# Reading the moving columns of all long matmuls as two alternating halves

## The chip, the core and the metric

The kernel runs on one core of one Trainium2 chip. TensorE multiplies, VectorE and ScalarE do elementwise work, GpSimd does a little of it and issues some transfers, SyncE issues most transfers, and 16 DMA engines move the data. The metric is the device time of one execution in microseconds (us). Before the change it is 2804.27 us, the median of three runs (2803.52 to 2804.97).

A TensorE product has two operands. The stationary one, 128 by 128 here and called the weights of the array, is loaded first; the moving one is streamed through column by column, and each of its columns gives one column of output in PSUM. The profile has a row for each of the two steps: LDWEIGHTS on "PEld", MATMUL on "PE".

## What is computed

One layer of a hybrid encoder trunk on 256 prompt tokens and 8 x 16 sample tokens, 384 in all, with a model width of 2048. In short:

```python
proj = rmsnorm(x) @ w_in                    # pool | z | xBC | dt | gates
a_pool = windowed means of pool - pool, mapped by pool_w, scaled by pool_scale
xbc = silu(causal_conv(xbc)); dt = softplus(dt_raw + dt_bias)
y, h = ssd_scan(xh, dt, A, Bm, Cm, h0)      # 64 heads, 8 groups
a_ssd = gated_rmsnorm(y + d_skip * xh, z)
merged = sigmoid(g_A) * (a_pool @ w_pool_proj) + sigmoid(g_B) * (a_ssd @ w_ssd_proj)
x = x + rmsnorm(merged @ w_out)
x = x + rmsnorm(square(relu(rmsnorm(x) @ w_up)) @ w_down)
```

All inputs and outputs are float32. The outputs are the new tokens and the new pool, convolution and SSD states of both groups.

## The kernel before

**Three matmuls for each product.** Each float32 operand is split into a rounded high part `h` (ScalarE, type fp32r) and the remainder `l` (VectorE, fp32r). A product is h·h + h·l + l·h, three matmuls that add up in the same PSUM columns. Each weight unit is a 128 x 1024 tile: SyncE fetches it (`wfetch`, L61), ScalarE and VectorE split it (`wsplit`, L70 and L71), and three such tiles are in flight.

**Two kinds of long product.** In the first, the tokens move: the output is a tile of 128 channels by 384 tokens, the stationary operand is a 128 x 128 block of weights, and the moving one is a tile of 128 input channels by 384 tokens. `mm3` (L82 to L85) issues the three matmuls, `half` (L91) runs eight such triples on one weight unit, `proj` (L111) runs two units into one PSUM tile. The columns of `w_in` for pool, z and xBC, the maps `pool_w`, the few columns for dt, and `w_up` go this way; `eprod` (L278) does the first four pool tiles while the inputs arrive, and `prod` and `prod_back` (L1128, L1146) the first `w_up` tiles, of which the first two are partly taken in pieces of 256 and 128 tokens.

In the second, the weights move: the output is 128 tokens by 512 channels, the stationary operand is a 128 x 128 block of tokens, and the moving one is 512 columns of a weight unit. `moving` (L117) runs these: in a unit there are two blocks of 128 rows, three token blocks and three matmuls, 18 in all (L125 to L127). The two gate parts of `w_in`, `w_pool_proj`, `w_ssd_proj`, `w_out` and `w_down` go this way. `_moving` (L1328) lays these weights out on the host.

**Stages.** Pool tiles and dt come first, then gate A and the pool output, then the SSD stage. That stage has eight groups of ten `proj` products (six for xBC, four for z), and between them come short SSD products in plain fp32 and fp32r (`t_trx`, `t_cb`, `t_Y`, `t_yi`, `t_pp`, `t_su`) which `lump` puts at set places in TensorE's order. Then follow gate B, the SSD output with the merging (`merge`, transposes at L916), `w_out`, and the MLP: in each of eight rounds eight `w_up` tiles and then four `w_down` blocks.

**Order.** Every engine runs its instructions in the order in which the program has them. `behind` ties an instruction behind another, `later` puts it behind the latest weight split, and `chain` ties consecutive products together. The program's tiles set the waits.

**Who reads the PSUM tiles of the first kind.** `pool_tile` multiplies by the token scale `rstd` into a window buffer (L355 for the 256 prompt tokens, L356 for the samples, each behind its 15 kept rows). `conv_in` writes into a buffer of 24 segments of 16 tokens, each behind 3 kept columns (L550). `zproj` multiplies by `rstd` (L881). `pool_map` scales and splits (L406, L407). The dt product is taken out at L448 and L450, and the `w_up` tiles at L1252. `proj` alternates two PSUM banks; the other products take turns in six.

Of the kernel before, what the change touches and what calls it, by code (L numbers as in the profile page):

```python
# [14 lines left out]
P = 128  # L15
T = 384
TP = 256
NB = 8
# [15 lines left out]
def build(ctx, tc, io):  # L34
# [44 lines left out]
    def wload(src, name):  # L79
        return wsplit(wfetch(src, name))  # L80

    def mm3(out, wh, wl, xh, xl, first, last, **how):  # L82
        te.matmul(out, wh, xh, start=first, stop=False, **how)  # L83
        te.matmul(out, wh, xl, start=False, stop=False, **how)  # L84
        return te.matmul(out, wl, xh, start=False, stop=last, **how)  # L85
# [31 lines left out]
    def moving(o, units, lhs, tail, done, pool=None, own=0, hook=None, mid=None):  # L117
        nk = 2 * len(units)
        n = len(units)

        def mm(b, wh, wl, k, k2):
            t = slice(b * P, b * P + P)
            c = slice(k2 * 512, k2 * 512 + 512)
            mh, ml = lhs[k][0][:, t], lhs[k][1][:, t]
            te.matmul(o[b], mh, wh[:, c], start=k == 0, stop=False)  # L125
            te.matmul(o[b], mh, wl[:, c], start=False, stop=False)  # L126
            last[0] = te.matmul(o[b], ml, wh[:, c], start=False, stop=k == nk - 1)  # L127

        for kp in range(n - tail):
            wh, wl = take(*units[kp])  # L130
            with behind(last[0] if chain[0] else None):
                for k2 in range(2):
                    for b in range(3):
                        mm(b, wh, wl, kp * 2 + k2, k2)
            if hook and kp in hook:
                hook[kp]()
        w = [wload(*units[kp]) for kp in range(n - tail, n - own)]
        for kp in range(n - own, n):
            f, name = wfetch(*units[kp])
            h = pool.tile([P, 1024], F32R, name=f"eh_{name}")  # L140
            l = pool.tile([P, 1024], F32R, name=f"el_{name}")
            s.activation(h, f, AF.Copy)
            v.tensor_tensor(l, f, h.bitcast(F32), ALU.subtract)
            w.append((h, l))
        for b in range(3):
            for i, (wh, wl) in enumerate(w):
                if mid and (b, i) in mid:
                    mid[b, i]()
                with behind(last[0] if mid else None):
                    for k2 in range(2):  # L150
                        mm(b, wh, wl, (n - tail + i) * 2 + k2, k2)
            done(b)
# [125 lines left out]
    def eprod(k, j, hl):  # L278
        h, l = hl
        col = lambda n: slice(j * 512 + n * P, j * 512 + n * P + P)  # L280
        xh, xl = xg[k]
        if k < 2:
            seq = [(0, h, xh), (0, h, xl)] if k == 0 else [(0, h, xh)]
            seq += [(n, h, xh) for n in range(1, 4)]
            seq += [(n, h, xl) for n in range(1 - k, 4)]
            seq += [(n, l, xh) for n in range(4)]
            for n, a, b in seq:
                with behind(last[0]):
                    last[0] = te.matmul(early[n], a[:, col(n)], b, start=k == 0 and a is h and b is xh, stop=False)
# [45 lines left out]
    with tc.tile_pool(name="phc", bufs=1, reuse_waits="tile") as pc, tc.tile_pool(name="phc2", bufs=2, reuse_waits="tile") as pc2:  # L335
# [12 lines left out]
        def pool_tile(gi, k4):  # L348
            w = WINDOWS[gi]
            k = gi * 4 + k4  # L350
            ps = early[k] if k < 5 else proj(in_units(1 + k), xg, f"p{k}")
            bf = bufs[k % 2]
            pv = bf[:, 15:271]
            sv = bf[:, 271:].rearrange("p (b t) -> p b t", b=NB)
            v.tensor_tensor(pv, ps[:, :TP], rstd[:, :TP], ALU.mult)  # L355
            v.tensor_tensor(  # L356
                sv[:, :, 15:],
                ps[:, TP:].rearrange("p (b t) -> p b t", b=NB),
                rstd[:, TP:].rearrange("p (b t) -> p b t", b=NB),
                ALU.mult,  # L360
            )
# [24 lines left out]
            v.tensor_tensor(d[:, :16], cur[:, 15:31], rc, ALU.mult)  # L386
            v.tensor_tensor(d[:, :16], d[:, :16], pv[:, :16], ALU.subtract)
            h = pc.tile([P, T], F32R, tag=f"dh{k4}", name=f"dh{k}", bufs=1)
            l = pc.tile([P, T], F32R, tag=f"dl{k4}", name=f"dl{k}", bufs=1)
            s.activation(h, d, AF.Copy)  # L390
            v.tensor_tensor(l, d, h.bitcast(F32), ALU.subtract)
            dd[gi][k4] = (h, l)

        def pool_map(gi, after=None):
            for hf in range(2):
                h, l = wload(io["pool_w"][gi, hf], f"pw{gi}_{hf}")
                for n2 in range(2):
                    n = gi * 4 + hf * 2 + n2
                    o = sstile(f"pw{n}")[:, :T]
                    with behind(after):  # L400
                        for k in range(4):
                            c = slice((n2 * 4 + k) * P, (n2 * 4 + k + 1) * P)
                            mm3(o, h[:, c], l[:, c], dd[gi][k][0], dd[gi][k][1], k == 0, k == 3)
                    ah, al = A[n]
                    sc = vec[:, V_PSC + n : V_PSC + n + 1]
                    s.activation(ah, o, AF.Copy, scale=sc)  # L406
                    v.scalar_tensor_tensor(  # L407
                        out=al, in0=o, scalar=sc, in1=ah.bitcast(F32), op0=ALU.mult, op1=ALU.subtract
                    )

        def gate_a(nb):
# [18 lines left out]
        def dt_phase(pb):  # L430
            ps = mmtile("pj_dt")[:, :T]
            for q in range(2):
# [5 lines left out]
                v.tensor_tensor(hl[:, :, 1], wv, hl[:, :, 0].bitcast(F32), ALU.subtract)  # L438
                for k in range(8):
                    c = hl[:, k].rearrange("p a n -> p (a n)")  # L440
                    te.matmul(ps, c, xg[q * 8 + k][0], start=q + k == 0, stop=False)
                    te.matmul(ps, c, xg[q * 8 + k][1], start=False, stop=q * 8 + k == KD - 1)
# [5 lines left out]
            with behind(s.copy(raw, ps[NH:])):  # L448
                s.activation(nA, alog, AF.Exp)
            v.tensor_tensor(raw, ps[:NH], raw, ALU.add)  # L450
# [78 lines left out]
    with tc.tile_pool(name="phd", bufs=2, reuse_waits="tile") as pd, tc.tile_pool(  # L529
# [15 lines left out]
        def conv_in(ui, c):  # L545
# [1 line left out]
            b = cbuf[ncv[0] % 3]  # L547
            ncv[0] += 1
            with later():
                v.tensor_tensor(b[:, :, 3:], seg(ps), seg(rstd), ALU.mult)  # L550
# [271 lines left out]
        for g in range(G + 1):  # L822
# [54 lines left out]
            def zproj(j):  # L877
                ps = proj(in_units(u0 + 6 + j), xg, f"z{g}_{j}")
                z = pd.tile([P, T], F32, tag="zs", name=f"zs{g}_{j}", bufs=7)
                with later():  # L880
                    v.tensor_tensor(z, ps, rstd, ALU.mult)  # L881
                    s.activation(z, z, AF.Silu)
                D.zs.append(z)

# [113 lines left out]
    with tc.tile_pool(name="phf", bufs=1, side="right", reuse_waits="tile") as pf, tc.tile_pool(  # L998
# [237 lines left out]
    with tc.tile_pool(name="phg", bufs=1, reuse_waits="tile") as pg, tc.tile_pool(  # L1236
# [9 lines left out]
        for c8 in range(NC):  # L1246
            hh = []
            for f8 in range(8):
                f = c8 * 8 + f8
                ps = ups[f] if f < 3 else proj([io["w_up"][f, 0], io["w_up"][f, 1]], xs2, f"up{f}")  # L1250
                t = pg2.tile([P, T], F32, tag="t", name=f"ht{f}")
                v.scalar_tensor_tensor(out=t, in0=ps, scalar=0.0, in1=r2, op0=ALU.max, op1=ALU.mult)  # L1252
# [163 lines left out]
```

## Time and profile before

| what | value |
|---|---|
| median of three runs | 2804.27 us |
| span of the profiled execution, first to last instruction | 2801.6 us |
| TensorE clock granted, mean | 0.999 |
| busy: TensorE matmul / weight load | 2791.7 / 2543.0 us |
| busy: VectorE / ScalarE / GpSimd | 1505.4 / 1171.9 / 135.1 us |
| matmuls | 15,269 |
| DMA traffic | 451.35 MB |

The device time of the profiled execution itself is not given apart from its span; the three timed runs have a median 2.7 us above that span. Rows of matmuls overlap, because one begins to stream while the one before still drains, and their ends are modelled; the distance between two starts is what a matmul costs in a full stream. The chain of waits is read in order of time, each piece with its start, its length and the number of instructions merged in it.

### The profile page before, as it was taken

What the parts mean: (1) busy time and instruction counts of PE and PEld (TensorE: products, weight loads), DVE (VectorE), ACT (ScalarE), POOL (GpSimd) and SP (SyncE); (2) the same over time, 40 slices, a digit from 0 to 9 for tenths busy, and PEclk for the clock granted to TensorE, in tenths of its full rate; (3) what the DMA queues carried; (4) which work ended last, traced back from release to release, by engine and by line L of the source; (5) the groups of instructions that cost most, each with busy time, mean ns of one, the idle gap of its engine ahead of it and who ended that gap; (6) DMA issues with size and microseconds to landing.
All of it is one profiled execution on the core that took longest, in us unless ns stands there. A gap on an engine that the chain in (4) does not pass through costs nothing.

```text
span 2801.6 us, 38313 instructions
## 1 busy us (share of the span) xinstructions
PE 2791.7 (100%) x15269; PEld 2543.0 (91%) x15269; DVE 1505.4 (54%) x1980; ACT 1171.9 (42%) x1820; POOL 135.1 (5%) x166
## 2 busy tenths in 40 slices
PE   9999999999999999999999999999999999999998
PEld 9998889999999999988888888989999898989897
DVE  6575335677787878756333336434444444444446
ACT  5443225556565646545222235433333332323233
POOL 0000000011110111010000000000000000000000
PEclk9999999999999999999999999999999999999999
DMA  7444445556565656657444544433433333333333
GB/s 264 141 126 146 139 141 198 186 189 218 186 223 191 210 192 213 207 190 241 162 149 155 183 142 132 131 132 124 131 126 129 127 128 128 128 128 127 129 126 127
DMA packets 146164, 451.35 MB, mean 161 GB/s; under 512 B 17921, under 2 KB 45121, under 8 KB 140993
## 3 DMA queue, kind: packets, MB, share of 16 engines
q1 hardware_dynamic: 134400, 389.90, 42.4%
q0 software_dynamic: 11584, 59.00, 5.6%
q8 instruction: 120, 1.97, 0.3%
q14 instruction: 60, 0.48, 0.1%
HBM read 407.11 MB, written 41.72 MB: 160 GB/s over the span
## 4 chain that ended last, share of the span: by engine, by line
PE 100%; DVE 0%; DMA 0%; ACT 0%; DVEq 0%; issue 0%
PE pj_up L83 6%; PE pj_up L85 6%; PE pj_up L84 6%; PE wd L126 6%; PE wd L127 6%; PE wd L125 6%; PE pj_x L83 5%; PE pj_x L84 5%; PE pj_x L85 5%; PE pj_z L83 3%; PE pj_z L84 3%; PE pj_z L85 3%; PE pj_sp L127 3%; PE pj_sp L125 3%; PE pj_sp L126 3%; PE pj_gb L125 2%
## 5 line engine op out<-in xcount | busy, mean ns | idle before, releaser
L83 PE MATMUL pj_up<-x1h,wh_up 128*128 128x384 f32 (+1 forms) x1024 | 342.0, 334 | 0.0
L85 PE MATMUL pj_up<-x1h,wl_up 128*128 128x384 f32 (+1 forms) x1024 | 341.7, 334 | 0.0
L84 PE MATMUL pj_up<-x1l,wh_up 128*128 128x384 f32 (+1 forms) x1024 | 341.7, 334 | 0.0
L127 PE MATMUL wd<-wh_wd,hl 128*128 128x512 f32 x756 | 294.2, 389 | 0.0
L126 PE MATMUL wd<-wl_wd,hh 128*128 128x512 f32 x756 | 294.2, 389 | 0.0
L71 DVE TENSOR_TENSOR wl_wd<-w_wd,wh_wd 128x1024 fp32r<-128x1024 f32 x126 | 154.4, 1226 | 260.2 <-ACT wh_wd L70 260.2
L125 PE MATMUL wd<-wh_wd,hh 128*128 128x512 f32 x756 | 294.1, 389 | 0.0
L70 ACT ACTIVATE wh_wd<-w_wd 128x1024 fp32r<-128x1024 f32 x126 | 134.0, 1063 | 347.3 <-PE wd L127 280.7
L70 ACT ACTIVATE wh_up<-w_up 128x1024 fp32r<-128x1024 f32 x126 | 134.0, 1063 | 321.8 <-PE pj_up L84 257.6
L71 DVE TENSOR_TENSOR wl_up<-w_up,wh_up 128x1024 fp32r<-128x1024 f32 x126 | 154.4, 1226 | 198.3 <-ACT wh_up L70 198.1
L83 PE MATMUL pj_x<-xgh,wh_x 128*128 128x384 f32 x768 | 258.2, 336 | 0.0
L84 PE MATMUL pj_x<-xgl,wh_x 128*128 128x384 f32 x768 | 256.6, 334 | 0.0
L85 PE MATMUL pj_x<-xgh,wl_x 128*128 128x384 f32 x768 | 256.5, 334 | 0.0
L84 PEld LDWEIGHTS pj_up<-x1l,wh_up 128*128 128x128 f32 x1024 | 192.2, 188 | 0.3
L83 PEld LDWEIGHTS pj_up<-x1h,wh_up 128*128 128x128 f32 x1024 | 192.2, 188 | 0.3
L85 PEld LDWEIGHTS pj_up<-x1h,wl_up 128*128 128x128 f32 x1024 | 192.2, 188 | 0.0
L83 PE MATMUL pj_z<-xgh,wh_z 128*128 128x384 f32 x512 | 171.0, 334 | 0.0
L84 PE MATMUL pj_z<-xgl,wh_z 128*128 128x384 f32 x512 | 171.0, 334 | 0.0
L85 PE MATMUL pj_z<-xgh,wl_z 128*128 128x384 f32 x512 | 171.0, 334 | 0.0
L127 PEld LDWEIGHTS wd<-wh_wd,hl 128*128 128x128 f32 x756 | 141.9, 188 | 29.4
L126 PEld LDWEIGHTS wd<-wl_wd,hh 128*128 128x128 f32 x756 | 141.9, 188 | 29.4
L125 PEld LDWEIGHTS wd<-wh_wd,hh 128*128 128x128 f32 x756 | 141.9, 188 | 29.3
(332 smaller groups left out, 5855.9 us busy)
## 6 DMA issues: line engine op xcount, KB each, us to landing
w_up<-w_up SPq DMA_DIRECT2D x128, 512.0 KB, 3.3
w_wd<-w_down SPq DMA_DIRECT2D x128, 512.0 KB, 3.3
w_x<-w_in SPq DMA_DIRECT2D x96, 512.0 KB, 3.5
w_z<-w_in SPq DMA_DIRECT2D x64, 512.0 KB, 3.5
w_sp<-w_ssd SPq DMA_DIRECT2D x64, 512.0 KB, 3.4
w_ga<-w_ga SPq DMA_DIRECT2D x32, 512.0 KB, 3.4
w_pp<-w_pp SPq DMA_DIRECT2D x32, 512.0 KB, 3.4
hs<-ssm POOLq DMA_DIRECT2D x16, 1024.0 KB, 6.7
```

The costliest lines, as they stand in the source:

```text
L70: cut[0] = s.activation(h, w, AF.Copy)
L71: cut[1] = v.tensor_tensor(l, w, h.bitcast(F32), ALU.subtract)
L83: te.matmul(out, wh, xh, start=first, stop=False, **how)
L84: te.matmul(out, wh, xl, start=False, stop=False, **how)
L85: return te.matmul(out, wl, xh, start=False, stop=last, **how)
L125: te.matmul(o[b], mh, wh[:, c], start=k == 0, stop=False)
L126: te.matmul(o[b], mh, wl[:, c], start=False, stop=False)
L127: last[0] = te.matmul(o[b], ml, wh[:, c], start=False, stop=k == nk - 1)
```

## The change

The moving operand of the long products is read in another order. An access pattern `woven` takes a tile of 2n columns as two halves and alternates between them by single columns: 0, n, 1, n + 1, and so on, which is a step of 192 elements for token tiles and of 256 for weights. The output pattern `pairs` is written in plain order, so PSUM column 2i holds column i and PSUM column 2i + 1 holds column n + i.

For the products in which weights move, the host lays the 512 columns of each block out so that the woven read yields them in their natural order; nothing else changes for their outputs. For those in which tokens move, the PSUM tile holds the tokens woven, and whoever reads it takes it with a stride of two (`even_odd`) and writes two halves (`halves`). In `pool_tile` the prompt's 256 tokens no longer lie in one such half, so three instructions stand in place of two (192, 64 and 128 tokens); in `conv_in` two stand in place of one. The two `w_up` tiles that are taken in pieces keep the plain order, as do the short SSD products.

```diff
@@ helpers
+    def woven(a):
+        return a.rearrange("p (a n) -> p n a", a=2)
+
+    def pairs(a):
+        return a.rearrange("p (n a) -> p n a", a=2)
+
+    def even_odd(a):
+        return a.rearrange("p (n a) -> p a n", a=2)
+
+    def halves(a):
+        return a.rearrange("p (a n) -> p a n", a=2)
+
+    def mm3w(out, wh, wl, xh, xl, first, last):
+        return mm3(pairs(out), wh, wl, woven(xh), woven(xl), first, last)
@@ half
-                ins = mm3(o, h[:, c], l[:, c], rhs[i][0], rhs[i][1], i == 0, i == len(rhs) - 1)
+                ins = mm3w(o, h[:, c], l[:, c], rhs[i][0], rhs[i][1], i == 0, i == len(rhs) - 1)
@@ moving
-            te.matmul(o[b], mh, wh[:, c], start=k == 0, stop=False)
-            te.matmul(o[b], mh, wl[:, c], start=False, stop=False)
-            last[0] = te.matmul(o[b], ml, wh[:, c], start=False, stop=k == nk - 1)
+            out, vh, vl = pairs(o[b]), woven(wh[:, c]), woven(wl[:, c])
+            te.matmul(out, mh, vh, start=k == 0, stop=False)
+            te.matmul(out, mh, vl, start=False, stop=False)
+            last[0] = te.matmul(out, ml, vh, start=False, stop=k == nk - 1)
@@ eprod
-            last[0] = mm3(early[n], h[:, col(n)], l[:, col(n)], xh, xl, False, k == KD - 1)
+            last[0] = mm3w(early[n], h[:, col(n)], l[:, col(n)], xh, xl, False, k == KD - 1)
...
@@ pool_tile
-            v.tensor_tensor(pv, ps[:, :TP], rstd[:, :TP], ALU.mult)
+            po = even_odd(ps)
+            v.tensor_tensor(pv[:, :192], po[:, 0], rstd[:, :192], ALU.mult)
+            v.tensor_tensor(pv[:, 192:], po[:, 1, :64], rstd[:, 192:TP], ALU.mult)
...
@@ pool_map
-                    s.activation(ah, o, AF.Copy, scale=sc)
+                    s.activation(ah, even_odd(o), AF.Copy, scale=sc)
...
@@ dt_phase
-                    te.matmul(ps, c, xg[q * 8 + k][0], start=q + k == 0, stop=False)
+                    te.matmul(pairs(ps), c, woven(xg[q * 8 + k][0]), start=q + k == 0, stop=False)
...
@@ conv_in
-                v.tensor_tensor(b[:, :, 3:], seg(ps), seg(rstd), ALU.mult)
+                for a in range(2):
+                    c12 = slice(a * 12, a * 12 + 12)
+                    v.tensor_tensor(
+                        b[:, c12, 3:],
+                        even_odd(ps)[:, a].rearrange("p (b t) -> p b t", b=12),
+                        seg(rstd)[:, c12],
+                        ALU.mult,
+                    )
@@ zproj
-                    v.tensor_tensor(z, ps, rstd, ALU.mult)
+                    v.tensor_tensor(halves(z), even_odd(ps), halves(rstd), ALU.mult)
@@ prod
+                        if n == 2:
+                            ins = mm3w(ups[n], w[0][:, c], w[1][:, c], xs2[k][0], xs2[k][1], k == 0, k == KD - 1)
+                            continue
@@ MLP
-                v.scalar_tensor_tensor(out=t, in0=ps, scalar=0.0, in1=r2, op0=ALU.max, op1=ALU.mult)
+                pv, tv, rv = (ps, t, r2) if f < 2 else (even_odd(ps), halves(t), halves(r2))
+                v.scalar_tensor_tensor(out=tv, in0=pv, scalar=0.0, in1=rv, op0=ALU.max, op1=ALU.mult)
@@ host
-    return np.ascontiguousarray(w.reshape(r // 256, 2, P, c // 512, 512).transpose(3, 0, 2, 1, 4)).reshape(c // 512, r // 256, P, 1024)
+    return np.ascontiguousarray(
+        w.reshape(r // 256, 2, P, c // 512, 256, 2).transpose(3, 0, 2, 1, 5, 4)
+    ).reshape(c // 512, r // 256, P, 1024)
```

More of the change, by code (lines that the diff above doesn't have):

```diff
@@ L288, in eprod @@
                 with behind(last[0]):
-                    last[0] = te.matmul(early[n], a[:, col(n)], b, start=k == 0 and a is h and b is xh, stop=False)
+                    last[0] = te.matmul(
+                        pairs(early[n]), a[:, col(n)], woven(b), start=k == 0 and a is h and b is xh, stop=False
+                    )
             return
         for n in range(4):
-            last[0] = mm3(early[n], h[:, col(n)], l[:, col(n)], xh, xl, False, k == KD - 1)
+            last[0] = mm3w(early[n], h[:, col(n)], l[:, col(n)], xh, xl, False, k == KD - 1)
     sx, hx, ax = (pa.tile([P, 3], F32, name=f"{n}x", bufs=1) for n in ("s", "h", "a"))
@@ L354, in pool_tile @@
             sv = bf[:, 271:].rearrange("p (b t) -> p b t", b=NB)
-            v.tensor_tensor(pv, ps[:, :TP], rstd[:, :TP], ALU.mult)
+            po = even_odd(ps)
+            v.tensor_tensor(pv[:, :192], po[:, 0], rstd[:, :192], ALU.mult)
+            v.tensor_tensor(pv[:, 192:], po[:, 1, :64], rstd[:, 192:TP], ALU.mult)
             v.tensor_tensor(
                 sv[:, :, 15:],
-                ps[:, TP:].rearrange("p (b t) -> p b t", b=NB),
+                po[:, 1, 64:].rearrange("p (b t) -> p b t", b=NB),
                 rstd[:, TP:].rearrange("p (b t) -> p b t", b=NB),
@@ L402, in pool_map @@
                             c = slice((n2 * 4 + k) * P, (n2 * 4 + k + 1) * P)
-                            mm3(o, h[:, c], l[:, c], dd[gi][k][0], dd[gi][k][1], k == 0, k == 3)
-                    ah, al = A[n]
+                            mm3w(o, h[:, c], l[:, c], dd[gi][k][0], dd[gi][k][1], k == 0, k == 3)
+                    ah, al = (halves(a) for a in A[n])
                     sc = vec[:, V_PSC + n : V_PSC + n + 1]
-                    s.activation(ah, o, AF.Copy, scale=sc)
+                    s.activation(ah, even_odd(o), AF.Copy, scale=sc)
                     v.scalar_tensor_tensor(
-                        out=al, in0=o, scalar=sc, in1=ah.bitcast(F32), op0=ALU.mult, op1=ALU.subtract
+                        out=al, in0=even_odd(o), scalar=sc, in1=ah.bitcast(F32), op0=ALU.mult, op1=ALU.subtract
                     )
@@ L440, in dt_phase @@
                     c = hl[:, k].rearrange("p a n -> p (a n)")
-                    te.matmul(ps, c, xg[q * 8 + k][0], start=q + k == 0, stop=False)
-                    te.matmul(ps, c, xg[q * 8 + k][1], start=False, stop=q * 8 + k == KD - 1)
+                    te.matmul(pairs(ps), c, woven(xg[q * 8 + k][0]), start=q + k == 0, stop=False)
+                    te.matmul(pairs(ps), c, woven(xg[q * 8 + k][1]), start=False, stop=q * 8 + k == KD - 1)
             n64 = lambda nm: pb.tile([NH, T], F32, name=nm)
@@ L447, in dt_phase @@
             nA = pb.tile([NH, 1], F32, name="nA")
-            with behind(s.copy(raw, ps[NH:])):
+            with behind(s.copy(halves(raw), even_odd(ps[NH:]))):
                 s.activation(nA, alog, AF.Exp)
-            v.tensor_tensor(raw, ps[:NH], raw, ALU.add)
+            v.tensor_tensor(halves(raw), even_odd(ps[:NH]), halves(raw), ALU.add)
             v.tensor_tensor(raw, raw, rstd[:NH], ALU.mult)
@@ L549, in conv_in @@
             with later():
-                v.tensor_tensor(b[:, :, 3:], seg(ps), seg(rstd), ALU.mult)
+                for a in range(2):
[5 more added lines that the diff above has]
+                        ALU.mult,
+                    )
             s.copy(b[:, 16:, :3], cst_[:, c, 1:])
```

## The prediction

> **What bounds the kernel now.** I read the page first (shares, clock, chain), then the waits of TensorE, the chain in order of time, the timeline, and groups kept apart by shape.
>
> ```profile
> span 2801.6 us, 38313 instructions
> ...
> PE 2791.7 (100%) x15269; PEld 2543.0 (91%) x15269; DVE 1505.4 (54%) x1980; ACT 1171.9 (42%) x1820; POOL 135.1 (5%) x166
> ...
> core 0: 2801.6 us, clock 0.999
> ...
> PE 100%; DVE 0%; DMA 0%; ACT 0%; DVEq 0%; issue 0%
> ...
> PE warm_o L213 <- DVE warm L209: 1.2, 1, 1.2
> ```
>
> TensorE works all the time at full clock, the chain is TensorE alone, and its only wait is 1.2 us at the start. So the time is a sum of distances from one matmul's start to the next, and whatever changes that distance changes the time one for one. A row's duration is no use for it, since rows overlap; the chain gives starts.
>
> ```profile
> 483.12 0.88 PE cb L598 x6
> 485.35 0.38 PE pj_x L83
> 527.17 0.71 PE py L651 x6
> 527.89 0.66 PE trx L608 x6
> ...
> 1481.87 1.31 PE tr_m L916 x12
> 1548.52 1.31 PE tr_m L916 x12
> ```
>
> Between the two `tr_m` rows lie the 1.31 us of transposes and 288 matmuls of 512 columns (16 weight units of 18): (66.65 - 1.31)/288 = 226.9 ns each. Between `pj_x` and `py` lie five products of 48 matmuls of 384 columns, the first taking 0.38: (41.82 - 0.38)/239 = 173.4 ns. The difference, 53.5 ns for 128 columns, is 0.418 ns a column; both widths leave 226.9 - 214.0 = 173.4 - 160.5 = 12.9 ns that no column explains. I call it the gap.
>
> ```profile
> L651 PE MATMUL py<-xhl,Bhl 128*128 128x256 f32 x90 | 13.1, 281 | 0.0
> L608 PE MATMUL trx<-cst,xs 128*128 128x128 f32 x96 | 13.1, 273 | 0.0
> L598 PE MATMUL cb<-xs,xs 128*128 128x128 f32 x32 | 4.9, 274 | 0.0
> L598 PE MATMUL cb<-xs,xs 128*128 128x256 f32 x16 | 4.8, 380 | 0.0
> ```
>
> The gap is not the same for all. `py`, fp32r like the long products and read as two blocks of 128: 0.71/6 = 118.3 ns, less 107.0 for 256 columns, gap 11.3. `cb` is plain fp32: four of 128 and two of 256 columns, 1024 in 0.88 us, which is two slots of 0.418 to a column (856 ns) and 24 ns over, a gap of 4 for each of six. `trx`: 768 columns, 642 of 660 ns, gap 3. Where columns come at half the rate, the gap is nearly gone. And it moves without any change of instruction:
>
> ```profile
> 1235.37 0.39 PE L126 MATMUL pj_gb<-wl_gb,xgh 128*128 128x512 f32 x1
> ...
> 1236.99 0.39 PE L127 MATMUL pj_gb<-wh_gb,xgl 128*128 128x512 f32 x1
> ```
>
> These two are seven starts apart, just after a break in the stream: 231.4 ns each, a gap of 17.4 for the instruction that elsewhere has 12.9. Beside every matmul runs the load of the next weights:
>
> ```profile
> 2001.42 0.33 PE L83 MATMUL pj_up<-x1h,wh_up 128*128 128x384 f32 x1
> 2001.43 0.19 PEld L84 LDWEIGHTS pj_up<-x1l,wh_up 128*128 128x128 f32 x1
> 2001.60 0.34 PE L84 MATMUL pj_up<-x1l,wh_up 128*128 128x384 f32 x1
> 2001.60 0.19 PEld L85 LDWEIGHTS pj_up<-x1h,wl_up 128*128 128x128 f32 x1
> ```
>
> I read these rows so: the gap is what the load of the next weights takes from the stream of moving columns, since it goes with the stream's rate, not with its length, and shifts when the two meet otherwise. That is inferred, not shown.
>
> **The change, part by part.** *No matmul is added or removed.* The busy time of lines 83, 125, 289 and 441 over the whole span, in this order, has their counts:
>
> ```profile
> 0.00:2802.00 2802.00, 875.34 (x2616) 490.93 (x2616) 1.00 0.48 161
> 0.00:2802.00 2802.00, 747.77 (x1920) 360.43 (x1920) 1.00 0.48 161
> 0.00:2802.00 2802.00, 5.69 (x24) 5.00 (x24) 1.00 0.48 161
> 0.00:2802.00 2802.00, 5.34 (x16) 3.00 (x16) 1.00 0.48 161
> ```
>
> Lines 84 and 85 go with 83, 126 and 127 with 125, 442 with 441. Of 3 x 2616 the early pieces of the first two `up` products stay as they are (24 of 256 columns, 72 of 384): 7848 - 96 + 24 + 32 = 7808 woven matmuls of 384 columns, and 3 x 1920 = 5760 of 512. Together 13,568 with 5.95 million columns, and a gap of 13,568 x 12.9 = 175 us: all that can be won. One ns a matmul is 13.6 us.
>
> *The reading order of the moving operand.* Consecutive columns now come from addresses 192 or 256 elements apart; the PSUM addresses are written in the same order as before. No row shows an fp32r matmul whose single columns jump. Bounds: the gap goes wholly (-175 us), or each column takes a second slot, as `cb` and `trx` show to be possible (+0.418 x 5.95 million = +2486 us). Nothing in the rows excludes either. I take the gap of `cb`, 4 ns, because the rows have no other small gap on products with changing weights, and because half the columns of one stream again come from each place: 12.9 - 4 = 8.9 ns won, 13,568 x 8.9 = 121 us. The weak point is that `cb` differs in its rate, not in its order. `trx`'s 3 ns would give 134 us; half the gap, 87.
>
> *PSUM taken out with stride two.*
>
> ```profile
> L1252 DVE SCALAR_TENSOR_TENSOR ht<-pj_up,r 128x384 f32<-128x384 f32 x64 | 35.6, 558 | 123.0 <-PE pj_up L85 122.1 <-ACT r L1233 0.7
> L550 DVE TENSOR_TENSOR cbuf<-pj_x,rstd 128x384 f32<-128x384 f32 x48 | 26.7, 556 | 49.4 <-PE pj_x L85 49.4
> L881 DVE TENSOR_TENSOR zs<-pj_z,rstd 128x384 f32<-128x384 f32 x32 | 17.8, 555 | 32.1 <-PE pj_z L85 32.1
> L407 DVE SCALAR_TENSOR_TENSOR al<-pw,vec,ah 128x384 fp32r<-128x384 f32 x16 | 9.6, 603 | 0.0
> L355 DVE TENSOR_TENSOR pbuf<-pj_p,rstd 128x256 f32<-128x256 f32 x16 | 6.8, 423 | 15.8 <-PE pj_p L85 15.8
> L356 DVE TENSOR_TENSOR pbuf<-pj_p,rstd 128x128 f32<-128x128 f32 x16 | 4.5, 283 | 0.0
> ```
>
> L355 and L356 give 1.09 ns a column and 143 ns an instruction. Splitting L550 in two costs 48 x 0.143 = 6.9 us of VectorE, one more piece in `pool_tile` 16 x 0.143 = 2.3. The stride itself costs between nothing and a second 1.09 ns a column, 0.42 us for each of some 170 reads, 72 us in all; a gain is excluded, for the instruction still makes one column at a time. I take nothing: VectorE is idle for 2801.6 - 1505.4 = 1296 us. TensorE feels it only if a bank is not free in time; `proj` alternates two banks and a product lasts 48 x 173.4 = 8.3 us, against at most 0.56 + 0.42 + 0.14 = 1.1 us of reading. ScalarE's L406 and L448 likewise.
>
> *Weights laid out on the host* change no transfer: same units, same bytes.
>
> *What a faster TensorE would wait for.*
>
> ```profile
> 490.00:1190.00 700.00, 700.00 (x4836) 683.44 (x4835) 540.76 (x728) 412.34 (x786) 90.69 (x90) 1.00 0.60 201
> 10.00:20.00 10.00, 10.00 (x57) 9.82 (x57) 6.97 (x10) 6.75 (x11) 0.00 (x0) 1.00 1.03 420
> ...
> w_wd<-w_down SPq DMA_DIRECT2D x128, 512.0 KB, 3.3
> ```
>
> In the SSD stage (first row) VectorE is busy 541 of 700 us; the weight splits have room. At the start (second row) the DMA engines are full, so I give back the gain of the first 240 matmuls, 2 us. In the MLP a unit of 18 matmuls would last 3.9 us, still above its 3.3 us transfer, and three are in flight.
>
> **Sum.** The shown runs' median, 2804.3, is 2.7 us above the profiled span, and I carry that. 2804.3 - 121 + 2 = 2685 us.
>
> [...]
>
> **The rivals.**
>
> *Half rate.* The moving stream may take several neighbouring columns in one read, as its steady 0.418 ns lets one think; with every column in another place each costs a read. Price 0.418 ns on 5.95 million columns: 2804 + 2486 = 5290 us. For it: `cb` and `trx` run at two slots a column, so the pace exists. Against it: a stream read in blocks (`py`) lost nothing, though its blocks are long. It decides from 0.02 ns a column on (121 us/5.95 million): then the gain is gone. [...]
>
> *A wider gap.* The same meeting of load and stream turns out worse. By the rows after the break, +4.5 ns: 13,568 x 4.5 = +61, 2865 us; a doubled gap gives 2979.
>
> *No effect.* The gap belongs to the change of weights and the order is indifferent: 2804, with the splits hidden. For it: the gap is equal for two widths. Against: 17.4 after a break.
>
> *Gain eaten in the SSD stage.* If VectorE's 541 of 700 us holds TensorE back, the 80 products' 3840 x 8.9 = 34 us stay: 2719.
>
> **How the numbers follow.** Narrower gap 0.56 (0.08 of it the eaten gain), no effect 0.06, wider gap 0.18, half rate 0.20. A measurement of this kernel tells about 0.2% (5.6 us) from no change: faster 0.56, same 0.06, slower 0.38. The likeliest case alone spans 2640 (nearly the whole gap) to 2760. Leaving half rate out, the range is 2640 to 2980, the doubled gap.
>
> **What would show it.** Right: chain distances near 164.5 and 218 ns, `py`, `cb` and `trx` unchanged, still no TensorE wait. Wrong: distances of 173 and 227 (no effect), above them by the same ns at both widths (wider gap), or by more at 512 than at 384 columns (a price by column: half rate). L550 twice 48 times at about 0.35 us says that the stride is free, 0.56 that it doubles. VectorE or DMA waits of TensorE between 490 and 1190 us would show eaten gain.

## The result and the profile after

The changed kernel takes 2657.98 us (median of four runs, 2657.36 to 2658.28) against 2804.32 us for the kernel before beside it: a ratio of 0.9477, 95% interval 0.9464 to 0.949. It is 146.3 us faster. The forecast was 2685 us, with 119 us gained.

From the page of the changed kernel, its share lines and one line of its DMA issues (queue, count, KB each, us to landing):

```profile
span 2655.6 us, 38356 instructions
PE 2645.0 (100%) x15269; PEld 2466.7 (93%) x15269; DVE 1503.8 (57%) x2044; ACT 1169.1 (44%) x1820; POOL 135.2 (5%) x166
PE 98%; DVE 1%; ACT 0%; DMA 0%; issue 0%; DVEq 0%; ACTq 0%
w_wd<-w_down SPq DMA_DIRECT2D x128, 512.0 KB, 3.2
```

The same 15,269 matmuls now fit into a span that is 146.0 us shorter. TensorE is still busy all the time; that 100% says nothing of the change, as a share of busy time can't say whether one matmul costs 216 or 227 ns. The chain in order of time does (start, length, what):

```profile
461.45 0.36 PE pj_x L98
500.65 0.72 PE py L678 x6
501.36 0.66 PE trx L635 x6
...
1405.45 1.31 PE tr_m L943 x12
1468.92 1.31 PE tr_m L943 x12
```

Read as before: (63.47 - 1.31)/288 = 215.8 ns for 512 columns, where it was 226.9; (39.20 - 0.36)/239 = 162.5 ns for 384, where it was 173.4. The column price is (215.8 - 162.5)/128 = 0.416 ns, unchanged, and the gap is 215.8 - 213.2 = 2.6 ns instead of 12.9. `py` (six in 0.72 us) and `trx` (six in 0.66), which the change leaves in plain order, cost what they did.

The terms add up: 5760 x 11.1 + 7808 x 10.9 = 149.0 us, 3.0 more than the span lost. Most of the difference is lost early. Up to the first `tk` product lie 288 woven matmuls of 512 columns and 992 of 384 (by the groups of that stretch), worth 288 x 11.1 + 992 x 10.9 = 14.0 us. The chain puts that product here, before and after:

```profile
243.90 0.83 PE tk L496 x11
...
232.06 0.83 PE tk L516 x11
```

So 11.84 us of the 14.0 arrived and 2.2 were lost. Distance by distance, against the steady ones of each kernel, about 1.1 us of this lie in the first 15 us, 0.8 at gate A near 66 us, and 0.35 in the `pool_w` products from 190 to 205 us. The waits of TensorE that only the changed kernel has (us in total, times, longest) make 0.7 us of it:

```profile
PE pj_ga L142 <- DVE wl_ga L71: 0.5, 1, 0.5
PE pj_p L305 <- ACT xgh L265: 0.2, 1, 0.2
```

The first of these is a weight split on VectorE that comes late for gate A. What is lost in the first 15 us has another reason. Two rows of the timeline before, then two after, of four matmuls of 384 columns each:

```profile
6.80 0.86 PE L289 MATMUL pj_p<-xgh,wl_e 128*128 128x384 f32 x4
7.49 0.85 PE L289 MATMUL pj_p<-xgh,wh_e 128*128 128x384 f32 x4
...
7.18 1.48 PE L305 MATMUL pj_p<-xgh,wl_e 128*128 128x384 f32 x4
8.46 1.07 PE L305 MATMUL pj_p<-xgh,wh_e 128*128 128x384 f32 x4
```

Before, the starts are 0.69/4 = 173 ns apart at this time; after, they are still 1.28/4 = 320 ns apart. In both traces distances of 320 ns end where the record of the granted clock begins at full speed, at 6.42 us before and at 8.97 us after. The chain gives the first 24 `pj_p` matmuls before, after, and in the experiment below in which only weights move in woven order, which leaves this stage as it was:

```profile
4.05 5.69 PE pj_p L289 x24
...
4.12 6.71 PE pj_p L305 x24
...
4.21 6.73 PE pj_p L296 x24
```

In plain order too they take 5.69 us in one trace and 6.73 in the other, so this part is chance and no price of the change. Nor is it all that delays the first `tk`: in the experiment on `py` below it starts at 231.93 us, only 0.13 earlier than here, and there the chain has, in place of these products, a transfer of the inputs, `xw`, from 2.60 us for 5.78 us, 48% of its first 12 us.

The readers of PSUM, in the groups kept apart by shape (count | busy us, mean ns of one | idle before them):

```profile
L1283 DVE SCALAR_TENSOR_TENSOR ht<-pj_up,r 128x384 f32<-128x384 f32 x64 | 35.6, 557 | 106.5 <-PE pj_up L100 105.7 <-ACT r L1263 0.6
L572 DVE TENSOR_TENSOR cbuf<-pj_x,rstd 128x192 f32<-128x192 f32 x96 | 29.6, 349 | 30.6 <-PE pj_x L100 30.6
L908 DVE TENSOR_TENSOR zs<-pj_z,rstd 128x384 f32<-128x384 f32 x32 | 17.7, 553 | 23.6 <-PE pj_z L100 21.8 <-DMA a_scr<-zs 1.8
```

557 ns with stride two where it was 558, 553 where it was 555: the stride costs nothing. The split in `conv_in` costs 96 x 349 - 48 x 556 = 6.8 us of VectorE, and TensorE doesn't wait for it. The SSD stage (window; us and counts of PE, PEld, DVE, ACT, POOL; clock; DMA share; GB/s):

```profile
470.00:1134.00 664.00, 664.00 (x4895) 646.97 (x4894) 542.67 (x773) 414.36 (x786) 92.18 (x92) 1.00 0.63 214
```

VectorE's 543 us of work now stand in 664 us rather than 700, and TensorE is never idle there.

### The profile page after: what moved, and what is told of

It is laid out like the page before. It is cut to its first block, busy times and chain, and to the rows that moved or that the text cites. A ratio compares the mean times of both kernels' runs of the same rounds, so it can differ in the third digit from the quotient of the medians.

```text
span 2655.6 us, 38356 instructions
## 1 busy us (share of the span) xinstructions
PE 2645.0 (100%) x15269; PEld 2466.7 (93%) x15269; DVE 1503.8 (57%) x2044; ACT 1169.1 (44%) x1820; POOL 135.2 (5%) x166
## 4 chain that ended last, share of the span: by engine, by line
PE 98%; DVE 1%; ACT 0%; DMA 0%; issue 0%; DVEq 0%; ACTq 0%
PE pj_up L99 6%; PE pj_up L98 6%; PE pj_up L100 6%; PE wd L143 6%; PE wd L142 6%; PE wd L141 6%; PE pj_x L98 5%; PE pj_x L99 5%; PE pj_x L100 5%; PE pj_z L99 3%; PE pj_z L98 3%; PE pj_z L100 3%; PE pj_sp L141 3%; PE pj_sp L143 3%; PE pj_sp L142 3%; PE pj_gb L141 2%
## 5 line engine op out<-in xcount | busy, mean ns | idle before, releaser
L98 PE MATMUL pj_up<-x1h,wh_up 128*128 128x384 f32 (+1 forms) x1024 | 333.9, 326 | 0.0
L100 PE MATMUL pj_up<-x1h,wl_up 128*128 128x384 f32 (+1 forms) x1024 | 333.7, 326 | 0.0
L99 PE MATMUL pj_up<-x1l,wh_up 128*128 128x384 f32 (+1 forms) x1024 | 333.7, 326 | 0.0
L141 PE MATMUL wd<-wh_wd,hh 128*128 128x512 f32 x756 | 286.5, 379 | 0.0
L142 PE MATMUL wd<-wl_wd,hh 128*128 128x512 f32 x756 | 286.5, 379 | 0.0
L143 PE MATMUL wd<-wh_wd,hl 128*128 128x512 f32 x756 | 286.5, 379 | 0.0
L98 PE MATMUL pj_x<-xgh,wh_x 128*128 128x384 f32 x768 | 251.9, 328 | 0.0
L99 PE MATMUL pj_x<-xgl,wh_x 128*128 128x384 f32 x768 | 250.4, 326 | 0.0
L100 PE MATMUL pj_x<-xgh,wl_x 128*128 128x384 f32 x768 | 250.4, 326 | 0.0
L71 DVE TENSOR_TENSOR wl_sp<-w_sp,wh_sp 128x1024 fp32r<-128x1024 f32 x64 | 78.4, 1224 | 154.0 <-ACT wh_sp L70 154.0
```

The source lines that it names most:

```text
L71: cut[1] = v.tensor_tensor(l, w, h.bitcast(F32), ALU.subtract)
L141: te.matmul(out, mh, vh, start=k == 0, stop=False)
L142: te.matmul(out, mh, vl, start=False, stop=False)
L143: last[0] = te.matmul(out, ml, vh, start=False, stop=k == nk - 1)
```

## Experiments

The change does what it was forecast to do, but more of it. Open was why: whether the load of the next weights is what the gap pays for, which part of the pattern matters (the order, the distance of the two places, the share of each), and whether the two kinds of product gain alike. In the runs that change the order, each of the six arrays of moving weights gets a pattern of its own, and the host lays its columns out to match, so one run holds six orders side by side. Unless a text says otherwise, rows are of 512 columns, and a distance is worked out from two rows of the timeline that are 30 starts apart. The granted clock is 0.999 in every one of these traces.

### Halves alternating in runs

```diff
@@ moving
-            out, vh, vl = pairs(o[b]), woven(wh[:, c]), woven(wl[:, c])
+            pat = PATS[units[0][1][:2]]
+            out, vh, vl = _plain(o[b], pat), _view(wh[:, c], pat), _view(wl[:, c], pat)
@@
+PATS = {'ga': ((2, 256), (1, 0)), 'gb': ((2, 128, 2), (1, 0, 2)), 'pp': ((2, 64, 4), (1, 0, 2)),
+        'sp': ((2, 32, 8), (1, 0, 2)), 'wo': ((2, 8, 32), (1, 0, 2)), 'wd': ((512,), (0,))}
```

The first part of an entry is the shape in which the 512 columns are seen, the second the order in which its axes are read: `((2, 128, 2), (1, 0, 2))` reads two columns of one half, two of the other, and so on.

> The changed kernel, but the weight-moving products alternate between their halves in runs of another length: gate A 1 column (as changed), gate B 2, pool output 4, SSD output 8, w_out 32, w_down plain order without alternation. Start-to-start distances of the 512-column matmuls, which were 226.9 ns plain and 215.8 woven. Theory 1 (each read of four neighbouring columns can collide with the weight load; single columns from two places avoid it): 215.8 for gate A, a step up as soon as four neighbours are read together, so gate B between 215.8 and 221, pool output and all longer runs 226 to 227, w_down 226.9. Theory 2 (any pattern with more than one dimension has the small gap): 215.8 for all but w_down; against it stands the product of two blocks of 128, which had 11.3 ns. Theory 3 (the gap shrinks with the number of jumps): a steady rise from 215.8 at 1 over about 221 at 8 to 226 at 32.

It took 2815.5 us (one run; the kernel before beside it 2803.0). Two of the orders in the timeline (start, length, engine and line, operation, names, shapes): runs of two in gate B at two places, and the plain order in `w_down`.

```profile
1240.13 0.50 PE L160 MATMUL pj_gb<-wh_gb,xgh 128*128 128x512 f32 x1
...
1250.13 0.50 PE L160 MATMUL pj_gb<-wh_gb,xgh 128*128 128x512 f32 x1
...
1261.25 0.51 PE L162 MATMUL pj_gb<-wh_gb,xgl 128*128 128x512 f32 x1
...
1271.45 0.51 PE L162 MATMUL pj_gb<-wh_gb,xgl 128*128 128x512 f32 x1
...
2285.31 0.39 PE L160 MATMUL wd<-wh_wd,hh 128*128 128x512 f32 x1
...
2292.11 0.39 PE L160 MATMUL wd<-wh_wd,hh 128*128 128x512 f32 x1
```

| columns in a run | 1 | 2 | 4 | 8 | 32 | plain |
|---|---|---|---|---|---|---|
| ns a matmul | 215.7 | 333.3 to 340.0 | 250.0 | 243.3 | 236.7 | 226.7 |

None of the theories on record gave this row. Only the alternation by single columns gains. By two columns it costs 107 to 113 ns more than plain (part of gate B runs at the one price, part at the other), and longer runs come back towards plain without reaching it. So it isn't that any alternation between two places helps, nor that all of them cost.

### Distance of the two places

```diff
+PATS = {'ga': ((64, 2, 4), (0, 2, 1)), 'gb': ((32, 2, 8), (0, 2, 1)), 'pp': ((16, 2, 16), (0, 2, 1)),
+        'sp': ((8, 2, 32), (0, 2, 1)), 'wo': ((4, 2, 64), (0, 2, 1)), 'wd': ((2, 2, 128), (0, 2, 1))}
```

> The changed kernel, but the two columns that alternate lie closer: gate A 4 columns apart (16 bytes), gate B 8, pool output 16, SSD output 32, w_out 64, w_down 128, with 256 in the changed kernel. Theory 1 (what matters is that neighbours in the stream are not neighbours in memory): 215.8 ns in all six. Rival (banks by address, the distance decides): 226.9 or more in some of them, 215.8 in others, with a border at a power of two. [...]

It took 2658.7 us. The nearest (gate A, 4 columns apart, in the order 0, 4, 1, 5, 2, 6, 3, 7) and the farthest (`w_down`, 128 apart) in the timeline:

```profile
296.88 0.38 PE L162 MATMUL pj_ga<-wh_ga,xgl 128*128 128x512 f32 x1
...
303.35 0.38 PE L162 MATMUL pj_ga<-wh_ga,xgl 128*128 128x512 f32 x1
...
2141.48 0.38 PE L160 MATMUL wd<-wh_wd,hh 128*128 128x512 f32 x1
...
2147.95 0.38 PE L160 MATMUL wd<-wh_wd,hh 128*128 128x512 f32 x1
```

Both are 6.47/30 = 215.7 ns, and the four distances between lie from 215.7 to 216.0. The distance doesn't matter from 16 to 512 bytes, in powers of two. That speaks against banks by address as the reason, which would show a border, and against a price that rises with the distance; neither is it a property of the halves.

### Steps, shuffles and more places

```diff
+PATS = {'ga': ((256, 2), (1, 0)), 'gb': ((128, 4), (1, 0)), 'pp': ((128, 2, 2), (0, 2, 1)),
+        'sp': ((4, 128), (1, 0)), 'wo': ((32, 16), (1, 0)), 'wd': ((8, 64), (1, 0))}
```

> The changed kernel, but other orders of reading: gate A every second column (8 bytes a step), gate B every fourth (16 bytes), pool output two columns apart and back (0, 2, 1, 3, so always within 16 bytes), SSD output four places in turn, w_out every sixteenth column, w_down eight places in turn. Theory 1 (four neighbours must not be read as one): 215.8 ns in all. [...]

It took 3766.9 us. Step two (gate A), the order 0, 2, 1, 3 inside each four columns (`w_pool_proj`), and four places in turn (`w_ssd_proj`), in the timeline:

```profile
366.17 0.63 PE L162 MATMUL pj_ga<-wh_ga,xgl 128*128 128x512 f32 x1
...
379.76 0.63 PE L162 MATMUL pj_ga<-wh_ga,xgl 128*128 128x512 f32 x1
...
430.34 0.39 PE L162 MATMUL pj_pp<-wh_pp,al 128*128 128x512 f32 x1
...
437.14 0.39 PE L162 MATMUL pj_pp<-wh_pp,al 128*128 128x512 f32 x1
...
1699.79 0.45 PE L161 MATMUL pj_sp<-wl_sp,abh 128*128 128x512 f32 x1
...
1708.29 0.45 PE L161 MATMUL pj_sp<-wl_sp,abh 128*128 128x512 f32 x1
```

| order | step 2 | step 4 | step 16 | 0, 2, 1, 3 | four places in turn | eight in turn |
|---|---|---|---|---|---|---|
| ns a matmul | 453.0 | 461.3 | 433.3 | 226.7 | 283.3 | 486.7 |

Half rate exists: step two costs 453.0 ns, twice the plain 226.7. It isn't the length of the jump from one column to the next that costs: with step two it is 8 bytes and the rate halves, while the woven order of the change, which jumps by about 1 KB with every column, is as fast as any (215.7).

One reading fits the second table and the distances, and part of the first table. *Suppose that every other column of the stream goes by a path of its own.* In the woven order each of the two paths then reads 0, 1, 2, 3, ..., so four successive columns of a path lie in one 16-byte piece: 215.7. In plain order a path reads 0, 2, 4, 6, two to a piece: 226.7. The order 0, 2, 1, 3 also leaves two to a piece (0 and 1, then 2 and 3 on the other path): 226.7. With step 2, 4 or 16 there is one to a piece: 453.0, 461.3, 433.3. The size of the piece follows from the runs: with two columns in it, plain order and step two would cost the same; with eight, the order with places 4 columns apart would cost what plain order does. In runs of two and with four or eight places a path hops between pieces with each column, and the prices lie between (333.3 to 340.0, 283.3) or above (486.7); for their sizes the reading has no number. Runs of 4, 8 and 32 it does not explain: a path then reads 0, 2, 256, 258 and so on, two to a piece as in plain order, and yet they cost 250.0, 243.3 and 236.7 instead of 226.7. The reading was formed after the two tables; the last experiment tests it.

### The load of the stationary operand

The prediction read the gap as the share of the next weights' load. With before's plain order, the load was made smaller or was spread out:

```diff
@@ moving (the order and all else as in the kernel before)
+            m = {"gb": 64, "pp": 32}.get(kind, P) if 0 < k < nk - 1 else P
+            out = o[b][:m]
+            mh, ml = mh[:, :m], ml[:, :m]
+            if kind == "sp":
+                mh, ml = (a[:, b:T:3] for a in lhs[k])
...
```

> The kernel before, plain moving order, with other weights of the array: gate B loads 64 stationary columns and pool output 32 in all but the first and last step of each sum (so most tokens of these two products miss most of their sum, and the outputs are not the reference's), SSD output takes every third token instead of 128 in a row (the tokens come out in another order, and what follows works on them as they are); gate A, w_out and w_down are as before. Distances, plain 226.9 ns for 512 columns, of which 213.3 to 214 are columns. Theory 1 (the gap is what the load takes from the stream): gate B about 220 to 221, pool output about 217, each with its share of the columns loaded; SSD output above 226.9, up to 253 if the price goes with 16-byte pieces (96 in place of 32). Rival (a fixed price of the plain order, whatever is loaded): 226.9 in all three.

It took 2818.5 us. The pool output with 32 stationary columns, gate B with 64, and `w_ssd_proj` with every third token, in the timeline:

```profile
346.75 0.39 PE L131 MATMUL pj_pp<-wh_pp,ah 128*32 128x512 f32 x1
...
353.70 0.39 PE L131 MATMUL pj_pp<-wh_pp,ah 128*32 128x512 f32 x1
...
1276.12 0.39 PE L133 MATMUL pj_gb<-wh_gb,xgl 128*64 128x512 f32 x1
...
1283.02 0.39 PE L133 MATMUL pj_gb<-wh_gb,xgl 128*64 128x512 f32 x1
...
1466.45 0.40 PE L132 MATMUL pj_sp<-wl_sp,abh 128*128 128x512 f32 x1
...
1473.52 0.40 PE L132 MATMUL pj_sp<-wl_sp,abh 128*128 128x512 f32 x1
```

64 columns: 230.0 ns; 32 columns: 231.7; every third token: 235.7; the untouched products: 226.7. A load of a quarter of the size doesn't shorten the distance but lengthens it by 5 ns. The theory that the gap is proportional to the load falls. That the loads matter at all in plain order (226.7 to 235.7) stays.

### One kind of product each

```diff
@@ only the products in which weights move keep the woven order: half, eprod, pool_map, dt, prod
-                ins = mm3w(o, h[:, c], l[:, c], rhs[i][0], rhs[i][1], i == 0, i == len(rhs) - 1)
+                ins = mm3(o, h[:, c], l[:, c], rhs[i][0], rhs[i][1], i == 0, i == len(rhs) - 1)
...
```

> One part of the change alone: the products in which weights move are woven and laid out on the host for it; the products in which tokens move, and everything that reads their PSUM, as before. If each matmul brings its own gain and nothing else has a price: 5760 x 11.0 ns = 63 us less than before, 2741 us. If the two parts hang together (a woven stream helping the next product of the other kind), less than 63 here and more than the rest in the other part.

```diff
@@ only the products in which tokens move keep the woven order: moving, _moving
-            out, vh, vl = pairs(o[b]), woven(wh[:, c]), woven(wl[:, c])
-            te.matmul(out, mh, vh, start=k == 0, stop=False)
+            te.matmul(o[b], mh, wh[:, c], start=k == 0, stop=False)
...
```

> The other part alone: tokens woven, PSUM read with stride two, weights that move in plain order as before. If each matmul brings its own gain: 7808 x 10.9 = 85 us less than before, about 2 us of it back at the start, 2720 us. If reading PSUM with stride two or the split instructions had a price on the path, less of a gain than that; rows of 0.35 us for the halves and 0.56 us for whole tiles say that they have none.

The first took 2740.92 us (ratio 0.9773, interval 0.9757 to 0.9789), the second 2720.02 (0.97, 0.9686 to 0.9715), both against 2804.7: 63.8 and 84.7 us gained, where 5760 x 11.1 = 63.9 and 7808 x 10.9 = 85.1 were due. Together they make 148.5, where the whole change gained 146.3 against its own runs of the kernel before. Both halves of the change earn by their number of matmuls, whatever the width. The loss of about 2 us is not tied to having both: in the traces the first `tk` comes at 241.50 and 234.86 us, 2.4 and 9.0 us earlier than before, where 3.2 and 10.8 were due. The medians, with a spread of up to 2 us, can't resolve it.

### Woven order with other loads, and both orders mixed

```diff
@@ moving (m, mh, ml as in the experiment on the load, the rest of the change kept)
+            orders = {"wd": (0, 1, 0), "wo": (1, 0, 1)}.get(kind, (1, 1, 1))
+            for i, ((st, mv), w2) in enumerate(zip(ways, orders)):
+                out, mv = o[b][:m], mv[:, c]
+                if w2:
+                    out, mv = pairs(out), woven(mv)
...
```

> The changed kernel with five of its products altered; the outputs are not the reference's. Gate B loads 64 stationary columns and pool output 32 in all but the first and last step (most tokens miss most of the sum); SSD output takes every third token; in w_down only the second of three matmuls is woven and in w_out only the first and third, so that sums add columns in two different orders. Theory of the load (it takes its share from the stream): sizes and steps of the load would show, as every third token did in plain order (235.9 ns). Theory of slack (the plain order is fetched no faster than it is used, so a fixed price at each start stays; the woven order is fetched faster and hides it): gate B, pool output and SSD output all 215.8 ns. For a triple: if each matmul has its own price, 215.8 + 2 x 226.8 = 669 ns in w_down and 2 x 215.8 + 226.8 = 658 in w_out; under the theory of slack a plain matmul may live on the lead of the woven one before it, so less than these, down to 647.

It took 2686.3 us. Gate B with 64 stationary columns, then `w_down`, where only the second matmul of each triple is woven, in the timeline:

```profile
1206.46 0.38 PE L151 MATMUL pj_gb<-wh_gb,xgl 128*64 128x512 f32 x1
...
1212.93 0.38 PE L151 MATMUL pj_gb<-wh_gb,xgl 128*64 128x512 f32 x1
...
2156.21 0.40 PE L151 MATMUL wd<-wh_wd,hh 128*128 128x512 f32 x1
2156.44 0.38 PE L151 MATMUL wd<-wl_wd,hh 128*128 128x512 f32 x1
2156.66 0.39 PE L151 MATMUL wd<-wh_wd,hl 128*128 128x512 f32 x1
...
2163.01 0.40 PE L151 MATMUL wd<-wh_wd,hh 128*128 128x512 f32 x1
```

In woven order the load has no effect: 64 columns 215.7 ns, 32 columns 216.0, every third token 215.7, where plain order had 230.0, 231.7 and 235.7. Mixed, `w_down`'s triple takes 6.80/10 = 680 ns, as much as three plain ones (3 x 226.7): the rows, whose starts have steps of 10 ns, put the woven one at 220 and the two plain ones at 230 each. `w_out`, with two of three woven, takes 667: 213, 217 and 237 in the mean of 12 triples. So each woven matmul has its own price, and each plain one pays more among woven ones. The theory of slack, in which neighbours share, predicted less than 669 and 658, and falls; a price of its own for each matmul gave just these two, 11 and 9 ns too little.

### The state product `py`

`py` is the only product with a gap like the long ones that the change leaves out. Its two blocks of 128 columns were read alternating:

```diff
-                        S.pp.rearrange("p (j n) -> p j n", j=2),
+                        S.pp.rearrange("p (n j) -> p n j", j=2),
...
-                        S.xhl[:, xl, :, b, :],
+                        S.xhl[:, xl, :, b, :].rearrange("p j n -> p n j"),
...
-            s.copy(pe.rearrange("p j n -> p (j n)"), S.pp)
+            s.copy(pe, S.pp.rearrange("p (n j) -> p j n", j=2))
```

> The changed kernel, and the product of the state of the prompt also takes its two blocks of 128 columns in turn (384 elements apart); its copy out of PSUM reads with a stride of two. If the price goes with single columns in one place and not with this kernel's long streams: 118.9 ns become 109 for each of 96 matmuls, about 1 us in all, 2657 us against 2658, at the edge of what can be told; the distances in the trace tell it. Rival (the short product is bound by its weight loads, 128 columns in 109 ns): no lower than 109 either, so 109 cannot tell these two apart, but 118.9 would speak against both.

It took 2657.64 us (ratio to the kernel before 0.9477, 0.9463 to 0.9491). Its chain:

```profile
500.63 0.67 PE py L678 x6
```

Six take 0.67 us instead of 0.72: 111.7 ns each, and the gap falls from 11.3 to about 4.7 ns. 96 x 6.6 ns = 0.6 us is all that can come of it, and in the time it can't be told from the changed kernel (2657.98). So the order works in a short product too; the last 2.7 ns down to the expected 109 stay open, and whether the weight loads bind there is not shown (`trx`, whose six loads are of 128 columns too, has its starts 0.66/6 = 110 ns apart).

### A test of the two paths

```diff
+PATS = {'ga': ((2, 128, 2), (2, 1, 0)), 'gb': ((2, 64, 4), (2, 1, 0)), 'pp': ((512,), (0,)),
+        'sp': ((2, 256), (1, 0)), 'wo': ((2, 256), (1, 0)), 'wd': ((2, 256), (1, 0))}
```

Gate A alternates between the halves with step two in each (0, 256, 2, 258, ...), gate B with step four (0, 256, 4, 260, ...). If the paths are right, the first has two columns of a path to a piece and costs what plain order does, the second one and costs what step two does.

> The changed kernel; gate A alternates between its halves but takes every second column of each (0, 256, 2, 258, 4, ...), gate B every fourth (0, 256, 4, 260, 8, ...), pool output is in plain order, the rest woven as changed. Theory of two paths (every other column of the stream goes by a path of its own; a path is at its best with four successive columns in one 16-byte piece, loses about 11 ns a matmul with two, and runs at half rate with one): on each path gate A has two columns a piece, like the plain order, so 226 to 228 ns, although every column jumps and the step is two, which without weaving cost 452; gate B has one, so 440 to 465; pool output 226.8. Rival (two open 16-byte pieces are kept, whichever columns they serve): gate A and gate B as the woven order, 215.8, since they alternate between two pieces only. Rival (any step other than one halves the rate): both 440 to 465.

It took 2807.2 us (the kernel before beside it 2804.07). Gate A and gate B in the timeline:

```profile
300.73 0.39 PE L162 MATMUL pj_ga<-wh_ga,xgl 128*128 128x512 f32 x1
...
307.53 0.39 PE L162 MATMUL pj_ga<-wh_ga,xgl 128*128 128x512 f32 x1
...
1291.10 0.63 PE L162 MATMUL pj_gb<-wh_gb,xgl 128*128 128x512 f32 x1
...
1304.69 0.64 PE L162 MATMUL pj_gb<-wh_gb,xgl 128*128 128x512 f32 x1
```

6.80/30 = 226.7 and 13.59/30 = 453.0 ns: the prices of plain order and of step two, as the two paths have it. Both rivals on record fall. The two paths remain an inference from timings; nothing in a trace shows them. A single path that compares each column with the one two places before it would cost the same, and the runs of 4, 8 and 32 columns stay unexplained.

## Why the prediction was right, and by how much it was off

**What bounds the kernel.** Right. The time is a sum of distances, and two distances and their counts give 149.0 us for the 146.0 that the span lost, and 2.2 of the 3.0 between them lie before the first `tk` product.

**The counts.** Right: 7808 and 5760. The two runs with one kind of product each gained 84.7 and 63.8 us, 10.8 and 11.1 ns for each of these.

**The reading order.** The direction was right, and the term mis-sized: "12.9 - 4 = 8.9 ns won, 13,568 x 8.9 = 121 us". Measured: 11.0 ns a matmul, 149 us. The step that failed is the choice of `cb`'s 4 ns for what would be left; 2.6 ns is left, at both widths (215.8 - 213.2 and 162.5 - 159.9). That choice leaned on a likeness ("half the columns of one stream again come from each place") to a product that, as the prediction says of its weak point, "differs in its rate, not in its order".

**The reason behind the gap.** Wrong in its form: "the gap is what the load of the next weights takes from the stream of moving columns". A load of a quarter of the size gave 231.7 ns where the full one had 226.7. In the woven order the load's size and step change nothing (215.7 to 216.0). What the runs support is that the price hangs on the order in which columns are read, and that loads and neighbours shift it (226.7 to 237) only while that order is plain. What makes up the 11 ns of plain order stays open.

**PSUM with stride two.** Right: 557 ns against 558; the split 6.8 us of VectorE against 6.9 forecast, hidden.

**What comes late next.** "I give back the gain of the first 240 matmuls, 2 us": 2.2 us were lost up to `tk`. The size was right partly by luck: 1.1 us of it is the 320 ns distance of the first matmuls, which lasted longer in this run than before, and 0.8 lies at gate A, whose new wait is for VectorE's weight split and not for a transfer. The run on `py`, whose first `tk` came only 0.13 us earlier and whose chain begins with 5.78 us of a transfer, points to the transfers of the inputs behind that, which is the reason that the prediction gave. The 3.2 us transfer of `w_down`'s units stayed hidden, as forecast.

**The rivals.** Half rate didn't come, but it exists close by: with step two instead of two halves a matmul costs 453.0 ns, and the whole run with such orders 3766.9 us. The rival let every jump to another place cost a read, and by that the woven order would have been slow; by the two paths the neighbours that count are every other column. `py`, read in long blocks, couldn't tell the two apart. A wider gap exists too, in runs of 4 to 32 columns (250.0 to 236.7 ns); whether it comes from load and stream meeting worse, as that rival had it, was not tested. No effect and the gain eaten in the SSD stage are excluded by the distances and by that stage's full TensorE row.

**The median over the span.** 2657.98 stands 2.4 us above 2655.6, where 2.7 were carried. The profiled run itself took 2657.36 us, 1.8 above its span; the rest is the spread of the runs.

## What to carry to other kernels

Where TensorE is the whole chain (100% of it before the change), read the distance between starts from the chain at two widths: the part that doesn't grow with the columns, 12.9 ns here, times the 13,568 matmuls, 175 us, was the author's estimate of the most that a change of order could win, and 149 us of it came. For fp32r moving operands, two places read alternately by single columns left 2.6 ns of that part's 12.9 here (215.8 instead of 226.9 ns for 512), with the places 16 bytes to 1 KB apart, and readers of PSUM at stride two paid nothing (557 ns against 558). A neighbouring order cost double (453.0 ns with step two), so an order is measured in the stream, one product at a time, before it is spread over a kernel.

## What the runs showed of the hardware that was not expected

- The order in which 512 fp32r columns are read sets a matmul's price between 215.7 and 486.7 ns, with the same data, the same loads and plainly written output.
- Plain order isn't the best: 226.7 ns, and up to 237 beside woven neighbours or with other loads. Alternation by single columns was the cheapest of the orders tried, 215.7 ns, and in it the load's size made no difference (215.7 to 216.0 with 32, 64 and 128 stationary columns).
- Alternating by two columns costs 333.3 to 340.0 ns, by one column 215.7; a step of two costs 453.0, but a step of two within alternating halves 226.7.
- Most of this fits two paths that take turns by column, each with 16-byte pieces: four successive columns of a path in a piece 216 ns, two 227, one 433 to 461. Runs of 4, 8 and 32 columns (250.0 to 236.7 instead of 227) don't fit, and for paths that hop between pieces the reading has no number. What the hardware does behind it was not shown, and no run writes PSUM in woven order to spare its readers the stride.
- The record of TensorE's full clock begins 6.42 us into the span before the change and 8.97 us after it. Until then matmuls of 384 columns start 320 ns apart or more, where 173 and 163 follow, while the mean granted clock of the span reads 0.999.
